# The output projection of a two-part trunk taken tile by tile, with norm, router and ranks behind each tile

## The chip, the cores and the metric

The kernel runs on one core of a Trainium2 chip. The metric is the device time of one execution in microseconds (us). The core has five engines that run their own instruction lists in order and wait for each other by semaphores: TensorE (PE, matmuls), VectorE (DVE), ScalarE (ACT), GpSimd (POOL) and SyncE (SP, which here issues most DMAs).

## The reference

One layer of a decoder trunk over 512 tokens of width 1024. A mixer `m` of three branches ends in a merged `y`, which goes through one output projection; then follow a LayerNorm, a router and a mixture of 16 experts, and a second LayerNorm:

```python
m = einsum('bse,ed->bsd', y, w_o) + b_o
x = layer_norm(ALPHA * x + m, ln1_g, ln1_b)
# hierarchical_moe
group_p = softmax(xf @ w_rg + b_rg)             # 4 groups, the best one
exp_logits = (xf @ w_re + b_re)                 # 4 experts in a group, the best two
gate = sum(one_hot(expert_id) * weights)        # (tokens, 16)
h = einsum('nd,edf->nef', xf, w_up); h_g, h_u = split(h, 2)
h = silu(h_g) * h_u * gate[:, :, None]
f = einsum('nef,efd->nd', h, w_down)
x = layer_norm(ALPHA * x + f, ln2_g, ln2_b)
```

## The kernel before

The 512 tokens are four tiles `t` of 128 rows (`NT` = 4). All large matmuls are done in three passes on operands that are split into a rounded part and a rest: ACT copies the rounded half (`hi`), DVE subtracts it from the source (`lo`).

The output projection has eight pieces `i`, a piece being one tile and one half of the columns, of 24 matmuls each: `wo_mm` (L787). `wo_add` (L794) adds the residual from PSUM on DVE, `wo_stats` takes the statistics of these 512 columns, `r_tr` (L804) transposes the piece on PE, `router` multiplies it with the router's weights. LN1 of a tile (`ln1_stats`, `center_ops`, `scale_ops`), its logits (`logits_a`, `logits_b`), the choice of group and experts (`route_ops`, which ends in the write of `cnt`), the ranks of the tokens within their experts (`rank_mm` on PE, `pos_ops` on DVE) and the selection of the first expert's tokens (`pick`, PE) need both halves of the tile. `put_x1` stores a finished tile to DRAM by two DMAs on SP, where the gathers (`gather`, L1082) of later experts fetch rows by index through POOL. `weave` alternates two lists of operations on an engine. The loop stands at L910; piece `i` is tile `i % 4`, column half `i // 4`.

Expert weights come as three units of 1 MB: 0 and 1 are the up weights, 2 the down weights. `load_unit` (L729) issues a unit on SP and picks its buffer by counting: up units go to the pool `rawx` (two buffers) or `o`, down units to `raw3` (one buffer) or `raw`. `prep_hi` and `prep_lo` (L756, L765) split the up weights into tiles of the pools `xp` and `hlp`, alternating by expert; `dn_hi` and `dn_lo` (L1198, L1203) split the down weights. Expert 0 here is the first in the order of work.

The experts are worked in 18 blocks (`for b in range(nb)`): up matmuls (`up_mm`, L1167), gate, transposes, down matmuls. The result of a block is scattered into one of two accumulators in DRAM, `acc_d[0]` and `acc_d[1]`, by POOL. The last blocks' results stay on the chip (`down_split`, into a tile of `xp`), and are added at the end.

At the end SP loads the rows of LN2's scale and shift into a `raw3` tile (L1388, issued in the last block but one), then three tiles of one accumulator (`acc_load`, L1241); POOL adds the other accumulator to them with DMAs (L1243); `combine` (L1440) adds the last blocks on PE and DVE (L1449), and LN2 follows. All engines run their lists in the order of the code; nothing is reordered at run time.

Of the kernel before, what the change touches and what calls it, by code (L numbers as in the profile page):

```python
# [9 lines left out]
F32 = mybir.dt.float32  # L10
# [43 lines left out]
def trunk(ctx, tc, x, mem, rows, cols, wz, wkv, pac, pb8, pb2, wax, ws, wo, wr, br, we, out):  # L54
# [650 lines left out]
    def load_xr(i):  # L705
        n, t = divmod(i, NT)
        xrs[i] = so2.tile([P, 512], F32, name="xr2") if i % 3 == 2 else so.tile([P, 512], F32, name="xr", bufs=2)
        act.dma_start(xrs[i], xr_d[t * P:(t + 1) * P, n * 512:(n + 1) * 512])
# [20 lines left out]
    def load_unit(key, u):  # L729
        if u < 2:  # L730
            c = counts["up"]
            counts["up"] += 1
            if c % 7 > 4 and key < E:
                t = mox.tile([P, 2048], F32, name="rawx", bufs=2)
            else:
                t = op_.tile([P, 2048], F32, name="o")
        else:
            c = counts["dn"]
            counts["dn"] += 1
            if c % 3 == 1 and key < E:  # L740
# [15 lines left out]
    def prep_hi(key, i):  # L756
        if i == 0:
            counts["prep"] += 1
            wus[key] = []
            pools[key] = xp if counts["prep"] % 2 and key < E else hlp  # L760
        t = pools[key].tile([P, 2, 1024], F32R, name="hl")
        act.copy(t[:, 0], raws[key, i // 2][:, (i % 2) * 1024:(i % 2 + 1) * 1024])  # L762
        wus[key].append(t)
# [18 lines left out]
    for e, u in ((1, 0), (1, 1), (1, 2), (2, 0), (2, 2)):  # L782
        load_unit(e, u)
# [3 lines left out]
    def wo_mm(i, ps, k0, k1):  # L787
        n, t = divmod(i, NT)
        for k in range(k0, k1):
            w = wos[2 * n + k // 4]  # L790
            c = max(t - 2, 0) * P
            mm3(ps, lambda s: yh[min(t, 2)][:, s, k, c:c + P], lambda s: w(s, k % 4), k == 0, k == KD - 1)

    def wo_add(i, ps):  # L794
        n, t = divmod(i, NT)
        dve.tensor_tensor(x1[:, t, n * 512:(n + 1) * 512], ps, xrs[i], op=ALU.add)

    def wo_stats(i):
        n, t = divmod(i, NT)
# [4 lines left out]
    def r_tr(i):  # L804
        n, t = divmod(i, NT)
# [7 lines left out]
    def router(i):  # L813
        n, t = divmod(i, NT)
# [95 lines left out]
    rest = []  # L910
    pending = {NT: [(2, 1)], NT + 1: [(3, 0), (3, 1)], NT + 2: [(4, 0)]}
    for i in range(2 * NT):
        j = i - 1
        t = j - NT
        ps = mmps()
        if i == 6:
            ohe = so2.tile([P, NT, P], F32, name="xr2")
        wo_mm(i, ps, 0, 2)
        if i:
            r_tr(j)  # L920
        if i in (NT + 1, NT + 2):
            for h in range(2):
                prep_hi(0, 2 * (i - NT - 1) + h)
        wo_mm(i, ps, 2, 4)
        if i:
            router(j)
        if t == 0:
            weave(ln1_stats(0))
        elif t == 1:
            weave(ln1_stats(1), scale_ops(0, 256, range(0, D, 256)))  # L930
            put_x1(sp, 0)
        elif t == 2:
            ops, r_ = route_ops(0, 2)
            rest += r_
            weave(ops, ln1_stats(2))
        if t >= 0:
            logits_a(t)
            weave(center_ops(t, D, (0,)))
            logits_b(t)
            if t:  # L940
                weave(scale_ops(t, 512, (0, 512)))
                put_x1(sp, t)
        wo_mm(i, ps, 4, 6)
        if t == 2:
            rank_mm(0)
            rank_mm(1)
            ops, r_ = route_ops(2, 3)
            rest += r_
            weave(ops, pos_ops(0, 2)[:2])
        wo_mm(i, ps, 6, 8)  # L950
# [54 lines left out]
    prep_hi(1, 0)  # L1005
    prep_hi(1, 1)
# [147 lines left out]
    load_unit(4, 1)  # L1154

# [154 lines left out]
    for b in range(nb):  # L1310
# [3 lines left out]
        if b == 0:  # L1314
            dn_hi(0, 0)
# [287 lines left out]
```

## Time and profile before

| | |
|---|---|
| median of three runs | 927.21 us (923.76 to 929.75) |
| profiled execution | 924.31 us, span 922.6 us |
| PE, DVE, ACT, POOL busy | 878.1, 586.4, 462.5, 91.2 us |
| mean DMA rate | 160 GB/s |
| output projection to expert 0 | 641 to 708.5 us |
| experts' blocks | to about 883 us |

A profile shows one execution; times in it are microseconds from the span's start. A row of a timeline gives start and length of an instruction (or of a run of alike ones, with their count), its engine, its line in the code and out<-in by the names of tiles, and in brackets the idle time of the engine before it with what ended it.

### The profile page before, as it was taken

To read this page: it belongs to the slowest core of one execution; us is meant where nothing else is said; L and a number is where in the kernel's file an instruction comes from. 1 tells how busy PE (TensorE), PEld (TensorE's weight loads), DVE (VectorE), ACT (ScalarE), POOL (GpSimd) and SP (SyncE) were. 2 spreads that over 40 slices of the span, in tenths; PEclk is the share of its full clock that TensorE was granted. 3 is DMA by queue.
4 is the path that set the end of the run, shared out by engine and by line. 5 is a ranking of instruction groups with operands and counts; after the bars stand their busy time and mean duration, and the time that the engine had idled before them with its cause. 6 is when DMAs were issued, how large, how long until landed. Compare 5 with 4: busy or idle time off the path is not lost.

```text
span 922.6 us, 11201 instructions
## 1 busy us (share of the span) xinstructions
PE 878.1 (95%) x4272; PEld 729.4 (79%) x4272; DVE 586.4 (64%) x995; ACT 462.5 (50%) x658; POOL 91.2 (10%) x86
## 2 busy tenths in 40 slices
PE   8999999999999999999999999999987889999990
PEld 5778888889998888888788888788866778888870
DVE  6755773344555543345866775765288987689966
ACT  5545432223454442215678687433124667679852
POOL 0000100000000100000000000000001123233943
PEclk9999999999999999999999999999999999999995
DMA  8313633323222612321313331338573888899582
GB/s 336 124 46 114 223 120 109 115 96 128 102 92 98 226 49 103 117 80 64 114 58 103 137 103 58 115 124 339 228 277 118 282 309 288 249 314 394 170 184 104
DMA packets 29871, 147.85 MB, mean 160 GB/s; under 512 B 5539, under 2 KB 5795, under 8 KB 16756
## 3 DMA queue, kind: packets, MB, share of 16 engines
q1 hardware_dynamic: 21316, 127.77, 37.8%
q0 software_dynamic: 7056, 17.12, 7.2%
q10 hardware_dynamic: 1440, 2.19, 0.7%
q8 instruction: 35, 0.57, 0.3%
q14 instruction: 24, 0.20, 0.1%
HBM read 137.29 MB, written 18.35 MB: 169 GB/s over the span
## 4 chain that ended last, share of the span: by engine, by line
PE 74%; DVE 11%; DMA 5%; ACT 4%; POOL 3%; issue 2%; SPq 0%; POOLq 0%; ACTq 0%; DVEq 0%
PE mm L109 60%; PE aux L109 4%; PE mm L307 3%; PE mm L1221 3%; DVE hl L768 2%; POOL rawx L1255 2%; DMA y<-acc_d 1%; DMA o<-in_we_dram 1%; DMA x<-in_x_dram 1%; DMA col<-in_cols_dram 1%; PE aux L1163 1%; DVE hl L83 1%; PE aux L463 1%; DMA acc_d<-yb,ix_x 1%; ACT hl L82 1%
## 5 line engine op out<-in xcount | busy, mean ns | idle before, releaser
L109 PE MATMUL mm<-hl 128*128 128x512 f32 x1416 | 327.7, 390 | 0.2 <-DVE hl L83 0.2
L109 PEld LDWEIGHTS mm<-hl 128*128 128x128 f32 x1416 | 264.6, 188 | 54.7 <-DVE hl L83 0.6
L83 DVE TENSOR_TENSOR hl<-raw,hl 128x1024 fp32r<-128x1024 f32 (+1 forms) x116 | 136.2, 1181 | 136.4 <-ACT hl L82 135.8
L82 ACT CAST hl<-raw 128x1024 fp32r<-128x1024 f32 (+1 forms) x116 | 116.3, 1014 | 126.1 <-PE mm L109 113.7
L109 PE MATMUL mm<-o,hl 128*128 128x512 f32 x624 | 142.9, 389 | 1.2 <-ACT o L82 1.2
L109 PEld LDWEIGHTS mm<-o,hl 128*128 128x128 f32 x624 | 117.1, 188 | 25.9 <-ACT o L82 1.6
L109 PE MATMUL mm<-hl,xs 128*128 128x512 f32 x432 | 105.1, 399 | 1.1 <-DVE xs L83 1.1
L109 PEld LDWEIGHTS mm<-hl,xs 128*128 128x128 f32 x432 | 80.7, 191 | 18.1 <-DVE xs L83 1.9
L768 DVE TENSOR_TENSOR hl<-o,hl 128x1024 fp32r<-128x1024 f32 (+1 forms) x52 | 57.8, 1143 | 2.0 <-ACT hl L762 1.9
L1221 PE MATMUL mm<-hl,hT 128*128 128x512 f32 x196 | 49.8, 400 | 0.8 <-DVE hT L83 0.8
L762 ACT CAST hl<-o 128x1024 fp32r<-128x1024 f32 x48 | 48.1, 1054 | 1.7 <-PE mm L1221 1.7
L1085 POOL DMA_INDIRECT y<-x_d,ixg x3 | 3.2, 1058 | 402.7 <-DVE rtl L1144 402.1
L1221 PEld LDWEIGHTS mm<-hl,hT 128*128 128x128 f32 x196 | 35.5, 188 | 7.9 <-DVE hT L83 1.2
L223 ACT ACTIVATE gate<-mm,col 128x512 f32<-128x512 f32 x24 | 16.5, 688 | 39.6 <-PE mm L109 39.5
L1210 DVE TENSOR_TENSOR hl<-raw,hl 128x1024 fp32r<-128x1024 f32 x26 | 30.8, 1225 | 3.5 <-PE mm L109 1.9
L1201 ACT CAST hl<-raw 128x1024 fp32r<-128x1024 f32 x32 | 31.9, 1053 | 0.0
L109 PE MATMUL mm<-memT,hl 128*128 128x256 f32 x192 | 27.3, 286 | 0.2 <-ACT memT L82 0.2
L810 ACT COPY x1T<-aux 128x512 f32<-128x512 f32 x8 | 4.7, 588 | 43.6 <-PE aux L809 23.6
L307 PE MATMUL mm<-o,hl 128*128 128x512 f32 x96 | 25.2, 409 | 1.1 <-ACT hl L82 0.4
L109 PEld LDWEIGHTS mm<-memT,hl 128*128 128x128 f32 x192 | 24.9, 191 | 0.9 <-ACT memT L82 0.4
L1085 POOL DMA_INDIRECT y<-x_d,ix_x x13 | 17.8, 1370 | 70.7 <-PE aux L1163 67.4
L109 PE MATMUL mm<-hl,yh 128*128 128x512 f32 x96 | 24.6, 400 | 0.0
(342 smaller groups left out, 1170.6 us busy)
## 6 DMA issues: line engine op xcount, KB each, us to landing
raw<-in_wz_dram SPq DMA_DIRECT2D x30, 1024.0 KB, 4.7
o<-in_we_dram SPq DMA_DIRECT2D x24, 1024.0 KB, 7.9
raw<-in_we_dram SPq DMA_DIRECT2D x16, 1024.0 KB, 6.6
raw<-in_pac_dram SPq DMA_DIRECT2D x8, 1024.0 KB, 4.6
raw<-in_wkv_dram SPq DMA_DIRECT2D x8, 1024.0 KB, 4.7
rawx<-in_we_dram SPq DMA_DIRECT2D x8, 1024.0 KB, 6.8
raw<-in_pb_dram SPq DMA_DIRECT2D x4, 1024.0 KB
raw<-in_wo_dram SPq DMA_DIRECT2D x4, 1024.0 KB, 4.8
```

Of the source, the lines that this page charges most:

```text
L82: act.copy(hi, src)
L83: dve.tensor_tensor(lo, src, hi.bitcast(F32), op=ALU.subtract)
L109: pe.matmul(ps, lhsT=a(sa_), rhs=b(sb_), start=first and i == 0, stop=last and i == 2)
L223: act.activation(store[j], ps, AF.Sigmoid, bias=cc(C_M + br_i * 8 + j))
L307: pe.matmul(ps, lhsT=xT(k, slice(t * P, (t + 1) * P))(sx), rhs=wv[2 * n + k // 4, k // 2 % 2][:, sw, k % 2, :], start=i == 0, stop=i == 23)
L762: act.copy(t[:, 0], raws[key, i // 2][:, (i % 2) * 1024:(i % 2 + 1) * 1024])
L768: (eng or dve).tensor_tensor(t[:, 1, c0:c1], src[:, c0:c1], t[:, 0, c0:c1].bitcast(F32), op=ALU.subtract)
L1085: pool.indirect_dma_start(out=xg, out_offset=None, in_=x1_d[:, :], in_offset=bass.IndirectOffsetOnAxis(ap=ix[:, b:b + 1], axis=0), bounds_ ...
L1201: act.copy(dnh[key][:, :, n * 512:(n + 1) * 512], dn_half(key, n))
L1210: eng.tensor_tensor(dnl[key][n], dn_half(key, n), dnh[key][:, :, ns].bitcast(F32), op=ALU.subtract)
L1221: pe.matmul(ps, lhsT=hT[:, sa_, f, :], rhs=dn[sb_][:, f, :], start=i + f == 0, stop=i + f == 3)
L1255: pool.tensor_scalar(t_[:, t * P:(t + 1) * P], iof, float(t * P), ixf, op0=ALU.add, op1=ALU.is_equal)
```

## The change

The pieces of the output projection are taken tile by tile: piece `i` is now tile `i // 2`, column half `i % 2`. The norm, the router's choice and the ranks of a tile follow the tile's second half, in the loop. Expert 0's raw up weights are loaded into the pool `raw`, and their rounded parts go to `o` tiles, one quarter in each of the iterations 1 to 4 (before: two quarters each in the iterations 5 and 6, `o` to `xp`). Before the loop SP loads only expert 0's units, the rows of LN1 and one unit of expert 1; four more units are issued in the iterations 4 and 5, and five behind the first expert's up matmuls. The rules by which `load_unit` and `prep_hi` choose a pool change their phase.

```diff
     def load_xr(i):
-        n, t = divmod(i, NT)
+        t, n = divmod(i, 2)
...
-            if c % 7 > 4 and key < E:
+            if key == 0:
+                t = rawp.tile([P, 2048], F32, name="raw")
+            elif c % 7 in (3, 4) and key < E:
                 t = mox.tile([P, 2048], F32, name="rawx", bufs=2)
...
-            if c % 3 == 1 and key < E:
+            if c % 3 == 0 and key < E:
                 t = mlate.tile([P, 2048], F32, name="raw3")
...
-            pools[key] = xp if counts["prep"] % 2 and key < E else hlp
-        t = pools[key].tile([P, 2, 1024], F32R, name="hl")
+            pools[key] = op_ if key == 0 else hlp if counts["prep"] % 2 or key >= E else xp
+        t = pools[key].tile([P, 2, 1024], F32R, name="hl" if key else "o")
...
-    for e, u in ((1, 0), (1, 1), (1, 2), (2, 0), (2, 2)):
-        load_unit(e, u)
+    load_unit(1, 0)
...
-    pending = {NT: [(2, 1)], NT + 1: [(3, 0), (3, 1)], NT + 2: [(4, 0)]}
+    pending = {4: [(1, 1), (2, 0)], 5: [(1, 2), (2, 2)]}
+
+    def ln1_tile(t, fill=()):
+        weave(ln1_stats(t), fill)
+        logits_a(t)
+        weave(center_ops(t, 512, (0, 512)))
+        logits_b(t)
+
+    def mm_pair(i, ps, q):
+        wo_mm(i, ps, 2 * q, 2 * q + 2)
+
     for i in range(2 * NT):
         j = i - 1
-        t = j - NT
         ps = mmps()
+        mm_pair(i, ps, 0)
...
         if i:
             r_tr(j)
-        if i in (NT + 1, NT + 2):
-            for h in range(2):
-                prep_hi(0, 2 * (i - NT - 1) + h)
-        wo_mm(i, ps, 2, 4)
+        if 0 < i < 5:
+            prep_hi(0, i - 1)
+        mm_pair(i, ps, 1)
         if i:
             router(j)
-        if t == 0:
-            weave(ln1_stats(0))
...
+        if i and i % 2 == 0:
+            t = i // 2 - 1
+            ln1_tile(t)
+            weave(scale_ops(t, 512, (0, 512)))
+            put_x1(sp, t)
+        if 0 < i < 5:
+            prep_lo(0, i - 1)
+        if i == 5:
+            ops, rest = route_ops(0, 2)
+            weave(ops)
+        mm_pair(i, ps, 2)
+        if i == 5:
             rank_mm(0)
             rank_mm(1)
...
+        if i == 6:
+            weave(pos_ops(0, 2) + rest)
+        if i == 7:
+            ops, rest = route_ops(2, 3)
+            weave(ops)
+        mm_pair(i, ps, 3)
         for e, u in pending.get(i, ()):
             load_unit(e, u)
+        if i == 7:
+            rank_mm(2)
         wo_add(i, ps)
         wo_stats(i)
-        if i in (NT + 1, NT + 2):
-            for h in range(2):
-                prep_lo(0, 2 * (i - NT - 1) + h)
...
     r_tr(2 * NT - 1)
-    rank_mm(2)
-    weave(ln1_stats(t), pos_ops(0, 2)[2:] + pos_ops(2, 3) + rest)
     pick(1, 0, 4)
+    prep_hi(1, 0)
+    prep_hi(1, 1)
     router(2 * NT - 1)
+    ln1_tile(t, pos_ops(2, 3))
     pick(1, 4, 8)
-    logits_a(t)
-    logits_b(t)
-    ops, rest = route_ops(t, NT)
-    weave(ops, center_ops(t, 512, (0, 512)) + scale_ops(t, 512, (0, 512)))
+    pick(2, 0, 8)
+    ops, rest3 = route_ops(t, NT)
+    weave(ops, scale_ops(t, 256, range(0, D, 256)))
     put_x1(sp, t)
-    pick(2, 0, 4)
     rank_mm(t)
-    pick(2, 4, 8)
     weave(pos_ops(t, NT))
     pick(t, 0, 8)
+    weave(rest)
+    rest = rest3
...
-    load_unit(4, 1)
...
         if b == 0:
+            for e, u in ((2, 1), (3, 0), (3, 1), (4, 0), (4, 1)):
+                load_unit(e, u)
             dn_hi(0, 0)
```

SP's list in the output projection, from the last load ahead of the loop. `in_we_dram` holds the expert weights, `x_d` the normed tiles, `acc_d` the first accumulator. Before:

```order
L751 DMA rawx<-in_we_dram 128x2048 x2
L751 DMA o<-in_we_dram 128x2048
L908 DMA x_d<-y 128x1024
L908 DMA acc_d<-y 128x1024
L908 DMA x_d<-y 128x1024
L908 DMA acc_d<-y 128x1024
L751 DMA o<-in_we_dram 128x2048
L908 DMA x_d<-y 128x1024
L908 DMA acc_d<-y 128x1024
L908 DMA x_d<-y 128x1024
L908 DMA acc_d<-y 128x1024
L751 DMA o<-in_we_dram 128x2048
```

Now:

```order
L753 DMA o<-in_we_dram 128x2048
L909 DMA x_d<-y 128x1024
L909 DMA acc_d<-y 128x1024
...
L753 DMA rawx<-in_we_dram 128x2048 x2
L753 DMA raw<-in_we_dram 128x2048 x2
L909 DMA x_d<-y 128x1024
L909 DMA acc_d<-y 128x1024
...
L753 DMA o<-in_we_dram 128x2048 x5
```

The stores of the first two tiles now stand ahead of the loads of the loop, and five loads follow the last store in a row.

DVE's list in the loop, from the addition of the seventh piece. Before (`hl<-o,hl` is expert 0's rounding, the L894 to L133 rows the variance of LN1, the rows from L851 the choice of experts):

```order
L796 TENSOR_TENSOR y<-mm,xr 128x512
L802 BN_STATS bnst_4874<-y 128x6
L768 TENSOR_TENSOR hl<-o,hl 128x1024 x2
L894 BN_AGGR bnmv<-bnst_4874 128x2
L851 TENSOR_TENSOR scr_4754<-ge 128x32
L124 TENSOR_SCALAR lnv_5133<-bnmv 128x1
L853 TENSOR_TENSOR scr_4754<-scr_4754,thr 128x32
L126 TENSOR_SCALAR lnr_5134<-lnv_5133 128x1
```

Now, from its addition of the seventh piece:

```order
L797 TENSOR_TENSOR y<-mm,xr 128x512
L803 BN_STATS bnst_5139<-y 128x6
L852 TENSOR_TENSOR scr_4746<-ge 128x16
L854 TENSOR_TENSOR scr_4746<-scr_4746,thr 128x16
L856 TENSOR_REDUCE rk<-scr_4746 128x4
...
L866 TENSOR_TENSOR cnt<-r_4750,goh 128x16
L797 TENSOR_TENSOR y<-mm,xr 128x512
L803 BN_STATS bnst_5139<-y 128x6
L895 BN_AGGR bnmv<-bnst_5139 128x2
```

Between the last two additions now stands only the choice of experts of one tile; the rounding and the norm that stood there have gone ahead.

SP's and DVE's lists at the end, with the numbers of the tiles. `raw3_6779` is the fourteenth expert's down weights, `raw_6969` and, in the change, `raw3_6972` the last one's; `in_rows_dram` holds the rows of LN2. SP before:

```order
L751 DMA raw3_6779<-in_we_dram 128x2048
...
L751 DMA raw_6873<-in_we_dram 128x2048
...
L751 DMA raw_6969<-in_we_dram 128x2048
L1388 DMA raw3_7103<-in_rows_dram 128x1024 x2
L1241 DMA y_7159<-acc1_d_96 128x1024 x3
```

DVE before:

```order
L1210 TENSOR_TENSOR hl_7066<-raw3_6779,hl_7064 128x2x512 x2
...
L1210 TENSOR_TENSOR o_7177<-raw_6969,hl_7174 128x2x512
L1178 SCALAR_TENSOR_TENSOR h_7179<-h_7179,gw_x_5891,mm_7131 128x256
L83 TENSOR_TENSOR rawx_6911<-aux_7189,rawx_6911 128x256
L1210 TENSOR_TENSOR o_7177<-raw_6969,hl_7174 128x2x512
```

SP now:

```order
L753 DMA raw3_6677<-in_we_dram 128x2048
...
L753 DMA raw_6876<-in_we_dram 128x2048
...
L753 DMA raw3_6972<-in_we_dram 128x2048
L1389 DMA raw3_7106<-in_rows_dram 128x1024 x2
L1240 DMA y_7162<-acc1_d_96 128x1024 x3
```

DVE now:

```order
L1209 TENSOR_TENSOR o_7173<-raw_6876,hl_7171 128x2x512 x2
L1209 TENSOR_TENSOR o_7180<-raw3_6972,hl_7177 128x2x512
L1177 SCALAR_TENSOR_TENSOR h_7182<-h_7182,gw_x_5894,mm_7134 128x256
L83 TENSOR_TENSOR rawx_6914<-aux_7192,rawx_6914 128x256
L1209 TENSOR_TENSOR o_7180<-raw3_6972,hl_7177 128x2x512
```

The single `raw3` buffer into which the rows of LN2 go was last read by DVE's rounding of the fourteenth expert, and is now last read by that of the last expert, at the end of DVE's rows above.

## Rows read from the trace of the kernel before

**Rows 1.** Windows: length, busy of PE, PEld, DVE, ACT, POOL (count), PEclk, DMA share, GB/s.
```profile
641.00:670.00 29.00, 29.00 (x156) 24.60 (x154) 7.10 (x18) 4.49 (x11) 0.00 (x0) 1.00 0.67 268
670.00:695.00 25.00, 19.25 (x106) 15.66 (x107) 22.52 (x73) 4.11 (x6) 0.00 (x0) 1.00 0.72 270
720.00:743.00 23.00, 18.73 (x94) 14.88 (x92) 22.62 (x61) 13.48 (x22) 3.60 (x2) 1.00 0.85 309
743.00:842.00 99.00, 99.00 (x484) 82.39 (x485) 79.89 (x98) 72.75 (x109) 30.52 (x21) 0.98 0.87 299
```

**Rows 2.** Timeline of PE, output projection and routing: start, length, what, [idle before].
```profile
640.58 0.60 PE L809 MATMUL aux<-ident,y 128*128 128x128 f32 x4
647.39 0.60 PE L809 MATMUL aux<-ident,y 128*128 128x128 f32 x4
683.76 0.66 PE L809 MATMUL aux<-ident,y 128*128 128x128 f32 x4 [2.06 <-DVE y L796]
689.25 1.63 PE L109 MATMUL mm<-hl,yh 128*128 128x512 f32 x6
703.32 4.39 PE L889 MATMUL mm<-xr,y 128*128 128x128 f32 x24
708.54 5.90 PE L109 MATMUL mm<-hl,xs 128*128 128x512 f32 x24
```

**Rows 3.** Timeline of DVE over the same stretch.
```profile
646.23 0.69 DVE L796 TENSOR_TENSOR y<-mm,xr 128x512 f32<-128x512 f32 x1 [5.39 <-PE mm L109]
668.16 0.21 DVE L894 BATCH_NORM_AGGREGATE bnmv<-bnst 128x2 f32<-128x12 f32 x1
670.10 1.28 DVE L899 SCALAR_TENSOR_TENSOR y<-y,bnmv,g 128x1024 f32<-128x1024 f32 x1
674.86 2.34 DVE L768 TENSOR_TENSOR hl<-o,hl 128x1024 fp32r<-128x1024 f32 x2
681.69 1.41 DVE L903 SCALAR_TENSOR_TENSOR y<-y,lnr,b 128x512 f32<-128x512 f32 x2
694.27 0.68 DVE L796 TENSOR_TENSOR y<-mm,xr 128x512 f32<-128x512 f32 x1
703.06 0.18 DVE L865 TENSOR_TENSOR cnt<-r,goh 128x16 bf16<-128x16 f32 x1
717.92 1.28 DVE L83 TENSOR_TENSOR xs<-aux,xs 128x512 fp32r<-128x512 f32 x2
```

**Rows 4.** Line L1085, the gathers: issue on POOL and time to landing, whole run.
```profile
L1085 POOL DMA_INDIRECT y<-x_d,ixg x3: 1001/1073/1099, 710.9 to 713.7; - x3
DMA to landing us min/median/max: 5.9/6.4/8.9
```

**Rows 5.** Timeline of PE: the second expert's transposes.
```profile
715.12 1.06 PE L1163 MATMUL aux<-ident,y 128*128 128x128 f32 x8 [0.69 <-DMA y<-x_d,ixg]
```

**Rows 6.** Timeline of SP, PE, ACT, DVE and POOL at the end of the kernel.
```profile
871.22 1.10 SPq L1388 DMA_DIRECT2D raw<-in_rows_dram  x2
873.74 1.28 SPq L1241 DMA_DIRECT2D y<-acc_d  x3
876.44 5.71 PE L109 MATMUL mm<-hl,xs 128*128 128x512 f32 x24
875.52 0.64 ACT L82 CAST hl<-mm 128x512 fp32r<-128x512 f32 x1
884.51 1.22 DVE L1210 TENSOR_TENSOR o<-raw,hl 128x1024 fp32r<-128x1024 f32 x1
885.78 1.88 POOL L1243 DMA_DIRECT2D y<-acc_d  x2 [4.97 <-DMA acc_d<-yb,ix_x]
891.65 0.69 DVE L1449 SCALAR_TENSOR_TENSOR y<-aux,y 128x512 f32<-128x512 f32 x1 [2.44 <-DMA y<-acc_d]
898.26 0.69 DVE L1449 SCALAR_TENSOR_TENSOR y<-aux,y 128x512 f32<-128x512 f32 x1 [2.67 <-DMA y<-acc_d]
```

**Rows 7.** Line L1241, the accumulator loads: time to landing.
```profile
DMA to landing us min/median/max: 6.5/6.5/6.5
```

More of the change, by code (lines that the diff above doesn't have):

```diff
@@ L787, in wo_mm @@
     def wo_mm(i, ps, k0, k1):
-        n, t = divmod(i, NT)
+        t, n = divmod(i, 2)
         for k in range(k0, k1):
@@ L794, in wo_add @@
     def wo_add(i, ps):
-        n, t = divmod(i, NT)
+        t, n = divmod(i, 2)
         dve.tensor_tensor(x1[:, t, n * 512:(n + 1) * 512], ps, xrs[i], op=ALU.add)
     def wo_stats(i):
-        n, t = divmod(i, NT)
+        t, n = divmod(i, 2)
         if n == 0:
@@ L804, in r_tr @@
     def r_tr(i):
-        n, t = divmod(i, NT)
+        t, n = divmod(i, 2)
         x1T = so.tile([P, 4, P], F32, name="x1T", bufs=1)
@@ L813, in router @@
     def router(i):
-        n, t = divmod(i, NT)
+        t, n = divmod(i, 2)
         ps = auxps()
@@ L825, in logits_b @@
     def logits_b(t):
-        dve.tensor_tensor(ge[:, t, :], ge[:, t, :], routed[NT + t][:, :20], op=ALU.add)
+        dve.tensor_tensor(ge[:, t, :], ge[:, t, :], routed[2 * t + 1][:, :20], op=ALU.add)
         dve.scalar_tensor_tensor(ge[:, t, :], ge[:, t, :], rstds[t], cv, op0=ALU.mult, op1=ALU.add)
@@ L908, in put_x1 @@
             eng.dma_start(d_[t * P:(t + 1) * P, :], x1[:, t, :])
-    rest = []
-    pending = {NT: [(2, 1)], NT + 1: [(3, 0), (3, 1)], NT + 2: [(4, 0)]}
+    pending = {4: [(1, 1), (2, 0)], 5: [(1, 2), (2, 2)]}
[6 more added lines that the diff above has]
+        wo_mm(i, ps, 2 * q, 2 * q + 2)
     for i in range(2 * NT):
         j = i - 1
-        t = j - NT
@@ L915, in trunk @@
         ps = mmps()
+        mm_pair(i, ps, 0)
         if i == 6:
             ohe = so2.tile([P, NT, P], F32, name="xr2")
-        wo_mm(i, ps, 0, 2)
         if i:
             r_tr(j)
-        if i in (NT + 1, NT + 2):
-            for h in range(2):
-                prep_hi(0, 2 * (i - NT - 1) + h)
-        wo_mm(i, ps, 2, 4)
+        if 0 < i < 5:
+            prep_hi(0, i - 1)
+        mm_pair(i, ps, 1)
         if i:
             router(j)
-        if t == 0:
-            weave(ln1_stats(0))
[L929 to L935, printed above, removed]
@@ L936, in trunk @@
-        if t >= 0:
-            logits_a(t)
-            weave(center_ops(t, D, (0,)))
-            logits_b(t)
[L940 to L944, printed above, removed]
+        if i and i % 2 == 0:
[8 more added lines that the diff above has]
+            weave(ops)
@@ L945, in trunk @@
+        mm_pair(i, ps, 2)
+        if i == 5:
             rank_mm(0)
             rank_mm(1)
[L947 to L950, printed above, removed]
+        if i == 6:
[4 more added lines that the diff above has]
+        mm_pair(i, ps, 3)
         for e, u in pending.get(i, ()):
             load_unit(e, u)
+        if i == 7:
+            rank_mm(2)
@@ L963, in trunk @@
     r_tr(2 * NT - 1)
-    rank_mm(2)
-    weave(ln1_stats(t), pos_ops(0, 2)[2:] + pos_ops(2, 3) + rest)
     pick(1, 0, 4)
+    prep_hi(1, 0)
+    prep_hi(1, 1)
     router(2 * NT - 1)
+    ln1_tile(t, pos_ops(2, 3))
     pick(1, 4, 8)
-    logits_a(t)
-    logits_b(t)
-    ops, rest = route_ops(t, NT)
-    weave(ops, center_ops(t, 512, (0, 512)) + scale_ops(t, 512, (0, 512)))
+    pick(2, 0, 8)
+    ops, rest3 = route_ops(t, NT)
+    weave(ops, scale_ops(t, 256, range(0, D, 256)))
     put_x1(sp, t)
-    pick(2, 0, 4)
     rank_mm(t)
-    pick(2, 4, 8)
     weave(pos_ops(t, NT))
     pick(t, 0, 8)
+    weave(rest)
+    rest = rest3
     rtl = rt0.tile([P, 7, NT], F32, name="rtl")
@@ L1004, in trunk @@
     ]
-    prep_hi(1, 0)
-    prep_hi(1, 1)
     weave(first)
```

## The prediction

> **What bounds the kernel now.** I read the stages first, by the windows of busy time [rows 1]. From 743 to 842, which is typical of the experts' blocks up to 883, TensorE (PE) is busy 99.00 of 99 us: whatever makes the first of these matmuls earlier makes the end earlier by as much, as long as nothing behind them is late. From 641 to 670, the first half of the output projection, PE is busy 29.00 of 29. Then from 670 to 695 only 19.25 of 25: here PE waits, and VectorE (DVE) is busy 22.52 of 25. From 720 to 743, expert maps and first experts, DVE has 22.62 of 23. So the program is bound by PE, with two stretches that belong to DVE, and its end, after 883, is a chain of waits over DMAs.
>
> The timeline of PE gives the loop's clock: the four transposes of one piece start at 640.58, those of the next at 647.39, a period of 6.81 us for the 24 matmuls of a piece with its small work [rows 2]. Where column half 1 brings norm and router, PE idles 2.06 before the transposes at 683.76, for DVE's addition (L796). The last six matmuls end at 689.25 + 1.63 = 690.88, but DVE adds the last piece only at 694.27 [rows 2, 3]: expert 0's rounding (2.34 for two), the norm and the ranks stand in its queue. The count of tile 3 ends at 703.06 + 0.18 = 703.24, and expert 0's first up matmul runs at 708.54 [rows 2, 3].
>
> At the end SyncE (SP) issues the rows of LN2 at 871.22 and three accumulator loads at 873.74, and GpSimd (POOL) adds the second accumulator with DMAs from 885.78; DVE waits for these before the first, 2.44 us at 891.65, and the third tile, 2.67 us at 898.26 [rows 6]. The loads of SP take 6.5 us to land [rows 7], so they lie at 873.74 + 6.5 = 880.2, 5.5 us before POOL wants them. That cover is the second thing that the change touches.
>
> **The output projection, tile by tile.** The 192 matmuls are the same; with the period 6.81 from 640.58, the transposes of the eighth piece stand at 640.58 + 7 x 6.81 = 688.25 if DVE keeps up. The addition starts 1.16 before the transposes (646.23 against 647.39 [rows 2, 3]), 0.69 of it its own, so DVE has a slack of 0.47 in each piece. DVE's work in an even iteration is now: addition 0.69 and the statistics of the same 512 columns, which I take alike; the variance chain 668.16 to 670.10, 1.94; the centring 1.28; three small operations on the logits at 0.18 (the row of the count is the nearest); the scaling 1.41; and one of expert 0's subtractions, half of 2.34 [rows 3]. That is 0.69 + 0.69 + 1.94 + 1.28 + 0.54 + 1.41 + 1.17 = 7.72, against 6.81: 0.91 too much, less the slack 0.47 is 0.44. It comes three times (iterations 2, 4, 6; the last has positions for the subtraction, which I count alike), 1.3 us. The odd iterations hold only the addition and a subtraction, or the ranks, and give DVE time to catch up. The eighth addition then starts at 688.25 - 1.16 + 1.3 = 688.4, not 694.27: **5.9 us earlier**. Bounds: 7.2 with no stall, and 1.0 if each of the three costs the 2.06 of idle time that the old order shows once [rows 2] (6.2 in all). I take 5.9, since DVE's own durations make it up.
>
> **From the eighth addition to expert 0.** The way over norm, router, logits and ranks of the last tile to its count took 694.27 to 703.24, 9.0 us. Its parts remain, with fewer filler operations between them; I take 9.0 again. From the count to expert 0's first matmul were 703.24 to 708.54, 5.3 us, held by the 24 selection matmuls of 4.39 [rows 2]. Now the eight of tile 2 go ahead of tile 3's count, so I take 4.4, with 3.8 and 5.3 as ends. Expert 0 starts at 688.4 + 9.0 + 4.4 = 701.8, **6.7 earlier**. The rounding of expert 1's first halves on ScalarE goes ahead too and costs nothing, since ScalarE is busy 13.48 of 23 even in the stretch behind [rows 1].
>
> **The loads.** Five units of 1 MB, 5.2 MB in all, now leave SP behind expert 0's matmuls instead of inside the loop; expert 0's units go to the raw pool and its rounded ones into "o" tiles, so these loads wait for PE's use of those tiles, up to 708. They meet the gather of expert 1's rows: issued at 710.9 before, with its transposes at 715.12, 4.2 later [rows 4, 5], hence issued at 704.2 now. DVE's subtraction of these rows came at 717.92 [rows 3], now due at 711.2. Gathers took 5.9, 6.4 and 8.9 us by the view of their line [rows 4]. With 6.4 and 1.2 for transposes (1.06) and cast, 704.2 + 6.4 + 1.2 = 711.8, **0.6 late**; the ends are 0 and 3.1 (at 8.9). Behind that, the stretch to 743 keeps its DVE work and PE its matmuls, so 6.7 - 0.6 = **6.1** arrives at the blocks. The unit (2,1), wanted by ScalarE at about 712, is issued near 703.5 and lands just in time; the other moved ones are wanted from 725 on.
> [...] The row with 8.9 shows that a gather may take 3 us longer than its neighbour, so I keep the range.
>
> **The end.** Now the parity: the units of the down weights that go to the single raw3 buffer are now the first, fourth, ... sixteenth instead of the second, ... fourteenth. So the last expert's down weights lie in the buffer into which LN2's rows are loaded next. Before, that buffer came free with the fourteenth's rounding, and SP issued at 871.22; now SP must wait for the second half of the last expert's rounding on DVE, 884.51 + 1.22 = 885.73 [rows 6]. I take 886.5: ScalarE's cast at 875.52 now writes into a tile that the last expert's up weights hold, and waits for six of the 24 matmuls from 876.44, up to 876.44 + 5.71 / 4 = 877.9 [rows 6]; of these 2.4 us the rounding, which has slack, gets a third. What is queued behind SP's wait: the three accumulator loads, since SP goes in order; and behind those POOL's adding loads; and behind those DVE. The sum, on the old time axis: rows issued from 886.5, 1.10 for two; first accumulator load at 887.6, landed 6.5 later [rows 7] at 894.1; POOL starts at 894.1 instead of 885.78, **8.3 later**. Everything from there to the end hangs on these DMAs (DVE waited for them with nothing else to do, at 891.65 and 898.26 [rows 6]), so all of it arrives. The lower end is 7.0: rows issued at 885.73 and a load that lands in 5.9, like the fastest gather [rows 4]. The upper is 9.7: the loads had a lead of 2.5 us over the rows ahead of them (871.22 to 873.74), now 1.1, and the other 1.4 is waited for.
> [...] The row has 6.5, and it is for this very load.
>
> **The sum.** The profiled execution took 924.31, with a span of 922.6 and 1.7 around it: 924.3 - 6.1 + 8.3 = 926.5. It lies 2.9 below the median of 927.21, so the forecast is 927.2 + 2.2 = **929** (rounded down from 929.4), with a range of its own from 926.5 to 935: front gain 2 to 7.5 (the ends of its terms don't all come together), loss 7.0 to 9.7. About 1%, 9.3 us, is what a measurement of this kernel can tell from no change, so this is "the same".
>
> **The rivals.**
> 1. The end costs nothing: the rows' load finds its buffer free, or the accumulators land while POOL still waits for the last scatter. For it: POOL did wait, 4.97 us, for a scatter [rows 6]. Against: that wait ended at 885.78, and SP can't issue before the rounding that ends there. Time 924.3 - 6.1 = 918.2, on the median 921. Chance 0.13.
> 2. Slower, by the burst of loads: the gather and the weights stand behind 5.2 MB, which at 299 GB/s [rows 1] take 17.5 us, up to 721. Expert 1's rows would come some 10 us after their due time 711.2, PE and DVE idle, and the gain of 6.7 becomes a loss of 3.3: 924.3 + 3.3 + 8.3 = 935.9, 939 on the median. It decides against the kernel when the gather lands over 6 us late. For it: the 8.9 us. Against: the gathers landed within 9 us though SP's loads ran beside them (309 GB/s from 720 to 743). Chance 0.12. [...]
> 3. The gain at the front doesn't come: DVE's queue holds the loop at every tile, and the old 694.27 is met again. Time 924.3 + 8.3 = 932.6, 935.5 on the median. Against: DVE's work in the loop isn't more than before, and PE ran 19.25 of 25. Chance 0.10.
>
> My forecast has the remaining 0.65.
>
> **How the numbers follow.** The range 920.5 to 937.5 takes in most of rival 1, rival 3 and the lower part of rival 2; about 0.17 is left out. Faster by over 1% (under 918) needs rival 1 with the front gain at its upper end or a term that I don't see: 0.08. Slower by over 1% (over 936.5): most of rival 2, and the upper part of rival 3: 0.15. Within 1%: 0.77.
>
> **What would show it.** The eighth addition at about 688.4 and expert 0's first matmul at 701.8; no idle time of PE over 1 us in the loop; the first gather landing by 711; steady blocks 6 us earlier. At the end, SP's rows issued only after the last rounding, near 880, the accumulator loads right behind, POOL's first adding load at about 894.1 - 6.1 = 888, and DVE waiting some 8 us more than before at the first combine. I am wrong if SP issues the rows early, if POOL's start doesn't move with the accumulators' landing, or if the front gain is outside 2 to 7.5.

## The result and the profile after

The changed kernel takes 932.95 us in the median of 20 runs (925.17 to 934.36), the kernel before 925.8 (20 runs, 923.39 to 929.75). The ratio is 1.0057, with a 95% interval from 1.0041 to 1.0072: slower by about half a per cent. The times of the changed kernel lie in two groups, fifteen between 931.9 and 934.4 and five between 925.2 and 929.1; that is why the ratio is smaller than that of the medians. In the longer group the mean granted clock of TensorE in each run is 0.975 to 0.977, in the shorter 0.978 to 0.980. The profiled execution took 932.28, with a span of 930.6, and belongs to the longer group.

The timeline of PE in the changed kernel, around the first experts (start, length, instruction, idle time before it):

```profile
640.49 0.60 PE L810 MATMUL aux<-ident,y 128*128 128x128 f32 x4
...
682.50 0.66 PE L810 MATMUL aux<-ident,y 128*128 128x128 f32 x4
...
701.17 5.75 PE L109 MATMUL mm<-o,xs 128*128 128x512 f32 x24
712.34 1.94 PE L1162 MATMUL aux<-ident,y 128*128 128x128 f32 x8 [5.42 <-DMA y<-x_d,ixg]
...
715.64 7.65 PE L109 MATMUL mm<-hl,xs 128*128 128x512 f32 x24
...
727.98 5.73 PE L109 MATMUL mm<-hl,xs 128*128 128x512 f32 x24
...
741.66 8.24 PE L109 MATMUL mm<-hl,xs 128*128 128x512 f32 x24
...
754.40 5.72 PE L109 MATMUL mm<-hl,xs 128*128 128x512 f32 x24
```

The same places in the kernel before that [rows 2, 5] don't have:

```profile
723.79 0.38 PE L1184 MATMUL aux<-ident,h 128*128 128x128 f32 x2
...
729.84 5.71 PE L109 MATMUL mm<-hl,xs 128*128 128x512 f32 x24
...
743.36 7.33 PE L109 MATMUL mm<-hl,xs 128*128 128x512 f32 x24
...
755.19 5.72 PE L109 MATMUL mm<-hl,xs 128*128 128x512 f32 x24
```

And on DVE, SP and POOL in the changed kernel: the eighth addition, tile 3's count, the burst of five loads, the gather of expert 1's rows, and DVE's subtraction of these rows:

```profile
688.25 0.69 DVE L797 TENSOR_TENSOR y<-mm,xr 128x512 f32<-128x512 f32 x1 [2.94 <-PE aux L878]
...
696.68 0.18 DVE L866 TENSOR_TENSOR cnt<-r,goh 128x16 bf16<-128x16 f32 x1
...
714.09 0.69 DVE L83 TENSOR_TENSOR xs<-aux,xs 128x512 fp32r<-128x512 f32 x1 [3.58 <-ACT xs L82]
```

```profile
702.86 5.28 SPq L753 DMA_DIRECT2D o<-in_we_dram  x5
703.39 1.10 POOL L1086 DMA_INDIRECT y<-x_d,ixg  x1 [394.74 <-ACT hl L764]
```

The loop did what was forecast. The transposes wait for DVE nowhere by much: the six periods from 640.49 to 682.50 take 42.0 us, 1.15 more than six times the 6.81 of [rows 2] (1.3 forecast), and the idle time of 2.06 at 683.76 in [rows 2] has gone. The eighth addition starts at 688.25 (688.4 forecast), the count ends at 696.86 (697.4) and expert 0's matmuls start at 701.17 (701.8; 708.54 in [rows 2]). So expert 0 is 7.37 us earlier. Then PE waits 5.42 us for the gather. DVE has expert 1's rows at 714.09, against 717.92 in [rows 3]: of the 7.37 there are 3.83 left. The reader should follow the same instruction in both kernels: the transposes after expert 1's matmuls stand at 723.13 now (0.16 before 715.64 + 7.65 = 723.29, since the two rows overlap) and at 723.79 before, 0.66 left; block 2 at 727.98 and 729.84, 1.86 (before, DVE held PE in between); block 3 at 741.66 and 743.36, 1.70; block 4 at 754.40 and 755.19, **0.79**. The matmuls of expert 1 took 7.65, where those of block 2 take 5.73, and those of block 3 8.24 instead of 7.33.

The windows tell why matmuls got longer (length, busy time of PE, PEld, DVE, ACT, POOL with counts, granted clock, DMA share, GB/s). Before:

```profile
712.00:728.00 16.00, 13.42 (x70) 10.61 (x69) 15.49 (x46) 9.40 (x15) 3.35 (x3) 1.00 0.81 267
743.00:752.00 9.00, 9.00 (x41) 7.54 (x42) 8.32 (x12) 5.15 (x7) 2.70 (x2) 0.81 0.81 274
```

After:

```profile
712.00:728.00 16.00, 14.98 (x65) 12.65 (x65) 11.94 (x34) 8.03 (x13) 1.00 (x1) 0.76 1.01 420
743.00:752.00 9.00, 9.00 (x41) 7.45 (x40) 6.66 (x9) 4.06 (x7) 2.26 (x3) 0.78 0.86 287
```

The granted clock behind PE's wait is 0.76 of full speed over 712 to 728, where it was 1.00. In steps of 2 us it is 1.00 up to 708, 0.87 from 708 to 710 and 0.50 from 710 to 718: here it falls while PE waits. From the transposes of expert 1 (712.34, before 715.12) to those behind its matmuls (723.13, before 723.79) the stretch takes 10.79 us at the lower clock, against 8.67: 2.1 of the 2.8 us that had been left, although PE waited 1.11 for DVE in that stretch before and doesn't now.

The end of the changed kernel, on SP, POOL and DVE, answers to [rows 6]:

```profile
886.09 0.81 SPq L1389 DMA_DIRECT2D raw<-in_rows_dram  x2
887.14 1.55 SPq L1240 DMA_DIRECT2D y<-acc_d  x3
```

```profile
893.38 1.92 POOL L1242 DMA_DIRECT2D y<-acc_d  x2 [13.37 <-DMA y<-acc_d]
```

```profile
884.81 1.22 DVE L1209 TENSOR_TENSOR o<-raw,hl 128x1024 fp32r<-128x1024 f32 x1
...
899.43 0.69 DVE L1450 SCALAR_TENSOR_TENSOR y<-aux,y 128x512 f32<-128x512 f32 x1 [9.91 <-DMA y<-acc_d]
```

In the chain that ended last, the first of the accumulator loads takes:

```profile
887.14 5.68 DMA y<-acc_d
```

SP issues the rows of LN2 at 886.09, where it was 871.22, right behind the rounding of the last expert on DVE (884.81 + 1.22 = 886.03); the accumulator loads follow at 887.14 instead of 873.74, and the first lands 5.68 later; POOL's first adding load moves from 885.78 to 893.38, 7.6 later, and DVE waits 9.91 at its first combine, where it waited 2.44. The span is 8.0 longer.

### The profile page after: what moved, and what is told of

It reads as the page before. It is cut to its first block, busy times and chain, and to the rows that moved or that the text cites. A ratio compares the mean times of both kernels' runs of the same rounds, so it can differ in the third digit from the quotient of the medians.

```text
span 930.6 us, 11201 instructions
## 1 busy us (share of the span) xinstructions
PE 883.3 (95%) x4272; PEld 733.2 (79%) x4272; DVE 588.8 (63%) x998; ACT 462.5 (50%) x658; POOL 89.8 (10%) x86
## 4 chain that ended last, share of the span: by engine, by line
PE 79%; DVE 11%; ACT 4%; DMA 3%; issue 2%; POOL 0%; SPq 0%; POOLq 0%; ACTq 0%; DVEq 0%
PE mm L109 62%; PE mm L1220 4%; PE aux L109 4%; PE mm L307 3%; DMA y<-acc_d 2%; PE aux L1162 2%; DMA y<-x_d,ixg 1%; ACT hl L82 1%; DVE hl L83 1%; PE mm L352 1%; PE aux L463 1%; DVE hl L770 1%; DVE lnr L126 1%; DVE th L687 0%; DVE o L1209 0%
## 5 line engine op out<-in xcount | busy, mean ns | idle before, releaser
L109 PE MATMUL mm<-hl 128*128 128x512 f32 x1416 | 327.6, 390 | 0.2 <-DVE hl L83 0.2
L109 PEld LDWEIGHTS mm<-hl 128*128 128x128 f32 x1416 | 264.6, 188 | 54.7 <-DVE hl L83 0.6
L109 PE MATMUL mm<-o,hl 128*128 128x512 f32 x624 | 142.9, 389 | 1.2 <-ACT o L82 1.2
L109 PEld LDWEIGHTS mm<-o,hl 128*128 128x128 f32 x624 | 117.1, 188 | 25.9 <-ACT o L82 1.6
L109 PE MATMUL mm<-hl,xs 128*128 128x512 f32 x408 | 101.7, 407 | 0.0
L109 PEld LDWEIGHTS mm<-hl,xs 128*128 128x128 f32 x408 | 78.6, 196 | 16.3
L770 DVE TENSOR_TENSOR hl<-o,hl 128x1024 fp32r<-128x1024 f32 (+1 forms) x45 | 50.5, 1151 | 4.8 <-ACT hl L764 4.7
L764 ACT CAST hl<-o 128x1024 fp32r<-128x1024 f32 x42 | 42.0, 1052 | 4.2 <-PE mm L1220 4.2
L109 PE MATMUL mm<-memT,hl 128*128 128x256 f32 x192 | 27.3, 286 | 0.2 <-ACT memT L82 0.2
L109 PEld LDWEIGHTS mm<-memT,hl 128*128 128x128 f32 x192 | 24.9, 191 | 0.9 <-ACT memT L82 0.4
L83 DVE TENSOR_TENSOR xs<-aux,xs 128x512 fp32r<-128x512 f32 x34 | 22.0, 686 | 5.4 <-ACT xs L82 5.4
L109 PE MATMUL mm<-hl,memT 128*128 128x256 f32 x192 | 24.3, 283 | 0.0
```

The lines of the kernel that those rows point to most:

```text
L83: dve.tensor_tensor(lo, src, hi.bitcast(F32), op=ALU.subtract)
L109: pe.matmul(ps, lhsT=a(sa_), rhs=b(sb_), start=first and i == 0, stop=last and i == 2)
L770: (eng or dve).tensor_tensor(t[:, 1, c0:c1], src[:, c0:c1], t[:, 0, c0:c1].bitcast(F32), op=ALU.subtract)
```

## The experiments

The theory after the result has two parts. **The end**: the rows of LN2 wait for the last expert's rounding, and the accumulator loads stand behind them on SP; price about 8. **The front**: the gain of 7.4 is real, but the gather of expert 1's rows meets the burst of five loads, and the clock is lower behind PE's wait for it; by block 4 they have eaten 6.6. That the wait is what brings the clock down is part of the theory, and the experiments don't show it. Rivals stand in the expectations. Ratios are to the kernel before, in the same runs.

**1. The last unit back in the raw pool**, in the changed kernel:

```diff
-            if c % 3 == 0 and key < E:
+            if c % 3 == 0 and c < 15 and key < E:
```

> The changed kernel, but the last expert's down weights go to the raw pool as they did before, so the single raw3 buffer comes free for the rows of LN2 after the thirteenth expert. Theory of the end (the rows' load waits for the last rounding, and the accumulator loads behind it): SP issues the rows near 862 to 871 instead of 886.1, POOL's first adding load goes back from 893.4 to about 885.2, and the time falls by 8.0, from 933.0 to 925. Rival (that wait is not what holds POOL, the last scatter is): POOL stays near 893 and the time within 1 us of 933.

Measured: 925.19 (10 runs, 923.7 to 926.7), ratio 0.9997 (0.9981 to 1.0013). SP and POOL at the end:

```profile
870.81 0.84 SPq L1389 DMA_DIRECT2D raw<-in_rows_dram  x2
872.88 1.34 SPq L1240 DMA_DIRECT2D y<-acc_d  x3
```

```profile
885.29 1.88 POOL L1242 DMA_DIRECT2D y<-acc_d  x2 [5.34 <-DMA acc_d<-yb,ix_x]
```

The 8 us come back, by an edit of one buffer's choice: the span is 922.7, 7.9 less than in the changed kernel's profile, and POOL's first adding load is 8.1 earlier. (By the ratios it is 0.6%, 5.6 us, since those of the changed kernel take in its shorter group.) The front is as in the changed kernel (expert 1's transposes at 712.18), so what is left of the change brings nothing that can be measured; the span before is 922.6.

**2. The other way round**: the kernel before with that rule alone.

```diff
-            if c % 3 == 1 and key < E:
+            if c % 3 == 0 and key < E:
```

> The kernel before with one rule of the change alone: raw3 takes the first, fourth, ... sixteenth down unit. Theory of the end: SP's rows of LN2 at about 885.7 instead of 871.2, POOL's first adding load at about 893.3 instead of 885.8, the time 925.8 + 7.6 = 933.4. Rival (the loss comes from the front or needs the moved parity of the up weights as well): 925.8, within 1 us.

Measured: 933.22 (4 runs, 931.2 to 935.1), ratio 1.0085 (1.0054 to 1.0116). With the old front:

```profile
885.26 0.81 SPq L1388 DMA_DIRECT2D raw<-in_rows_dram  x2
886.31 1.47 SPq L1241 DMA_DIRECT2D y<-acc_d  x3
```

```profile
892.71 1.88 POOL L1243 DMA_DIRECT2D y<-acc_d  x2 [12.44 <-DMA y<-acc_d]
```

The rule alone makes the loss, 6.9 us here by the medians and the profiles, 7.9 by the ratio; neither the front nor the parity of the up weights is needed.

**3. What is it that waits?** In the changed kernel the accumulator loads go to SP ahead of the rows, which still wait.

```diff
-            load_gb(sp, 0)
-            load_gb(sp, 1)
...
     acc_load((nb + 1) % 2, 2, sp)
+    load_gb(sp, 0)
+    load_gb(sp, 1)
```

> The changed kernel with the three accumulator loads issued on SP ahead of the two loads of LN2's rows; the rows still wait for the last rounding in the same buffer. Theory of the end (it is the loads queued behind the wait that cost, not the late rows): accumulator loads near 873, POOL's first adding load near 885.3 instead of 893.4, the rows at 886 land by 893, before POOL's first use of them near 898; the time 925, like the kernel with the last unit in the raw pool. Rival (the late rows themselves delay LN2): 928 to 933.

Measured: 927.41 (10 runs, six at 927.3 to 928.6 and four at 920.8 to 923.4), ratio 0.9996 (0.9968 to 1.0023).

```profile
873.06 2.26 SPq L1240 DMA_DIRECT2D y<-acc_d  x3
886.20 0.82 SPq L1389 DMA_DIRECT2D raw<-in_rows_dram  x2
```

```profile
885.28 1.88 POOL L1242 DMA_DIRECT2D y<-acc_d  x2 [5.16 <-issue]
...
898.63 0.86 POOL L1242 DMA_DIRECT2D y<-acc_d  x1 [10.02 <-DMA y<-acc_d]
```

POOL's first adding load is back at 885.28. So most of the loss is the queue behind the wait. But the rows, two loads of 512 KB, now leave at 886.20, in the stretch of POOL's own loads (from 885.28 on): the last adding load starts at 898.63 after a wait of 10.02, where the first experiment has 895.88 and 7.25. With the same front (expert 1's transposes at 712.32 and 712.18) the span is 925.8, 3.1 more than there, and the median is 2.2 more. The expectation was right about POOL's start; the rival, that the late rows cost something themselves, holds for the smaller part.

**4. The burst later**, in the changed kernel: SP reads the table of experts' numbers first, which DVE has ready at 708.2.

```diff
         if b == 0:
+            regs[NSTAT] = sp.value_load(blk["eid"][0:1, 0:1], min_val=0, max_val=E - 1)
             for e, u in ((2, 1), (3, 0), (3, 1), (4, 0), (4, 1)):
                 load_unit(e, u)
```

> The changed kernel, but SP reads the table of experts' numbers (ready at 708.2) before the five loads of 1 MB behind expert 0's matmuls, so they leave at about 708.5 instead of 702.9. Theory of the gather (the burst holds expert 1's rows back): the gather's transposes stand some 4.2 after its issue, at about 707.6 instead of 712.3, PE's idle time of 5.4 falls under 1.5, expert 1's matmuls start at 710 to 711 instead of 715.6, and nearly the whole 7.4 of the front arrives at the blocks: the time falls by 6 to 7, to 926 to 927. Rival one (DVE's maps and rounding up to 743 decide, the gather hides there): PE's idle time goes but the time falls by at most 2, to 931. Rival two (the gather is slow by itself, here because its rows were just stored): transposes stay near 712, time 933.

Measured: 927.77 (10 runs, 926.7 to 929.1), ratio 1.0017 (1.0002 to 1.0033), 5.2 less than the changed kernel's median. The gather of expert 1's rows on POOL, PE, and the window of the clock:

```profile
704.19 1.10 POOL L1086 DMA_INDIRECT y<-x_d,ixg  x1 [395.70 <-DVE rtl L1145]
```

```profile
701.84 5.89 PE L109 MATMUL mm<-o,xs 128*128 128x512 f32 x24
708.84 1.06 PE L1162 MATMUL aux<-ident,y 128*128 128x128 f32 x8 [1.11 <-DMA y<-x_d,ixg]
...
711.96 8.03 PE L109 MATMUL mm<-hl,xs 128*128 128x512 f32 x22 [0.57 <-DVE xs L83]
...
724.67 5.74 PE L109 MATMUL mm<-hl,xs 128*128 128x512 f32 x24
```

```profile
712.00:728.00 16.00, 15.32 (x61) 12.22 (x62) 14.03 (x46) 8.60 (x13) 1.80 (x2) 0.82 0.98 398
```

The wait is down to 1.11. From the gather's issue to the transposes of its rows it is 4.65 us (704.19 to 708.84), against 8.95 in the changed kernel (703.39 to 712.34) and 4.2 before [rows 4, 5]. Block 2 starts 5.2 earlier than before (729.84). Rivals one and two fall. The times lie in one group. In this execution the clock is low again in expert 1's matmuls, 8.03 for 22 of them, and less arrives than the 6 to 7 expected. It is 0.87 over 695 to 712 and 0.82 over 712 to 728, and PE's waits before these matmuls are 1.11 and 0.57: here the clock fell without a wait of 5.4.

**5. Both edits** (1 and 4).

> Both edits together. If the two losses stand apart, their sum: 933.0 - 8.0 - 6.5 = 918.5, a ratio of 0.992 to the kernel before. If the loads that leave later are missed by the rounding behind, or the front's gain is lost again in the blocks: 922 to 925.

Measured: **919.26** (6 runs, 917.2 to 920.2), ratio 0.9925 (0.9902 to 0.9948), faster than both kernels. PE, and the window of the clock:

```profile
700.99 5.73 PE L109 MATMUL mm<-o,xs 128*128 128x512 f32 x24
708.03 1.06 PE L1162 MATMUL aux<-ident,y 128*128 128x128 f32 x8 [1.31 <-DMA y<-x_d,ixg]
...
711.04 5.29 PE L109 MATMUL mm<-hl,xs 128*128 128x512 f32 x22 [0.59 <-DVE xs L83]
...
722.63 5.73 PE L109 MATMUL mm<-hl,xs 128*128 128x512 f32 x24
```

```profile
712.00:728.00 16.00, 14.00 (x67) 11.10 (x67) 15.29 (x46) 9.77 (x15) 1.62 (x1) 1.00 1.01 418
```

7.2 us of the front arrive at block 2, and the median is 7.0 below that of the kernel before. The gather is as in experiment 4; here the 22 matmuls take 5.29 at a clock of 1.00. That is the price of the clock by two rows with nearly the same waits (why it fell in one of the two is not shown): 8.03 - 5.29 = 2.7 on PE, of which some 1.2 reach block 2 (2.04 less the 0.85 that expert 0 was later), since PE at full clock waits 1.21 for ScalarE instead. The two losses add, by the medians: 932.95 - 7.8 - 5.2 = 920, measured 919.3.

**6. How the gather is slowed.** Two of the five loads at once, three after the table:

```diff
         if b == 0:
-            for e, u in ((2, 1), (3, 0), (3, 1), (4, 0), (4, 1)):
+            load_unit(2, 1)
+            load_unit(3, 0)
+            regs[NSTAT] = sp.value_load(blk["eid"][0:1, 0:1], min_val=0, max_val=E - 1)
+            for e, u in ((3, 1), (4, 0), (4, 1)):
                 load_unit(e, u)
```

> The changed kernel with two of the five loads behind expert 0's matmuls at once and three after the table of experts' numbers (708.2). Theory of the gather: its wait grows with the bytes that are queued when it starts, so 2 MB (5 us at the 400 GB/s of that stretch) from 702.9 let the rows land at about 709 to 710, between the 708.8 without and the 712.3 with all five loads; PE idles 2 to 3, and the time is 927.5 to 930. Rival (any load of SP ahead of the gather holds it as long as five do): transposes at 712, 933.

Measured: 932.25 (10 runs, three at 925.4 to 926.5 and seven at 931.2 to 935.5), ratio 1.0048 (1.0019 to 1.0078): the expectation by bytes was wrong. The gather, issued at 705.24, keeps PE waiting as long as with all five:

```profile
714.31 1.94 PE L1162 MATMUL aux<-ident,y 128*128 128x128 f32 x8 [5.53 <-DMA y<-x_d,ixg]
```

The DMA queues show what moved. In the changed kernel, from 708 to 710, SP's queue (q1) and POOL's (q0) have these packets, MB and shares of the DMA engines' time:

```profile
q1 hardware_dynamic: 59, 0.48, 60.2%
q0 software_dynamic: 67, 0.27, 32.9%
```

In this step and the next two, both queues moved about as many packets (78 and 80 from 710 to 712, 75 and 74 from 712 to 714). By these figures a packet of the gather carries 0.27 MB / 67 = 4 KB and one of the weights 0.48 MB / 59 = 8 KB, and POOL's queue moved 0.27, 0.27 and 0.30 of 0.75, 0.82 and 0.87 MB, about a third; in experiment 4, with nothing of SP's beside it, it moved 0.54 MB from 706 to 708. In experiment 6 itself the numbers are 63 and 69 from 710 to 712, but 81 and 41 in the step before and 56 and 122 in the step after, and in the changed kernel they are 78 and 27 from 706 to 708, so equal numbers are not shown as a rule. Here SP's queue moved 0.11, 0.58, 0.53, 0.52 and 0.35 MB in steps of 2 us from 704 to 714, so its first two loads, 2.1 MB, took until about 714 (the other three left from 711.0 on, behind them), and the gather landed 8.9 after its issue, at 714.1. That two loads hold the gather as long as five because they last as long as it does is the author's reading of these steps.

**7. One load at once, four later**, the same edit with (2, 1) alone ahead of the table.

> The changed kernel with one of the five loads (2,1) at once and four after the table of experts' numbers. In the half burst the gather was as late as with all five, so the bytes queued are not what counts. Theory of the share (while SP's queue has packets, POOL's queue moves about a third of the bytes, and all of them once SP's is empty): 1 MB is through near 707.5, the gather shares for some 2 us only and its transposes stand at 709 to 710, PE idles 1.5 to 2.5, the time is 927.5 to 929.5. Rival (any load of SP in front makes the gather late by 4): transposes at 712, 932 to 933.

Measured: 926.83 (10 runs, six at 925.5 to 927.1 and four at 929.8 to 930.7), ratio 1.0032 (1.0013 to 1.0051). None of the ten times lies in the 927.5 to 929.5 that the share gave; the rival's 932 to 933 falls. The profile, of the shorter group, doesn't test the share, but shows another thing, on PE, SP and POOL:

```profile
701.89 7.40 PE L109 MATMUL mm<-o,xs 128*128 128x512 f32 x24
709.13 1.03 PE L1162 MATMUL aux<-ident,y 128*128 128x128 f32 x8
```

```profile
704.83 6.30 SPq L753 DMA_DIRECT2D o<-in_we_dram  x5
```

```profile
703.42 1.10 POOL L1086 DMA_INDIRECT y<-x_d,ixg  x1 [394.87 <-DVE rtl L1145]
```

Here expert 0's matmuls ran at a lower clock (0.80 over 695 to 712), 7.40 us instead of 5.75. The first load waits for PE to finish with a tile (in the changed kernel's trace SP waits 5.4 us for L109 before it), and so left at 704.83 instead of 702.86, behind the gather at 703.42; and the gather's rows were there without a wait. So here the slow PE let the gather go first. What that is worth in time is not shown, since no execution of the longer group was profiled.

**8. PE kept busy in the wait**, in the changed kernel: 22 more matmuls of expert 0's rows with themselves, into a tile that nobody reads.

```diff
+            wps = auxps()
+            for k in range(22):
+                pe.matmul(wps, lhsT=xsm[0][:, 0, k % 8, :], rhs=xsm[0][:, 0, 0:4, :].rearrange("p k n -> p (k n)"), start=k == 0, stop=k == 21)
             transp(1)
```

> The changed kernel with 22 extra matmuls of 128x512 (on expert 0's rows, into a tile that nobody reads) between expert 0's matmuls and expert 1's transposes, some 5.2 us in which PE waits for the gather anyway. Theory of the clock (the wait brings the granted clock down, and expert 1's work then runs at the lower one: transposes 1.94 instead of 1.06, matmuls 7.65 instead of 5.72): the granted clock from 712 to 728 is 1.00 instead of 0.76, the matmuls of expert 1 take about 5.7, and the time falls by 2 to 4, from 933 to 929 to 931. Rival (the clock falls for another reason, or DVE's work hides it): the clock or the time stays, 932 to 934.

Measured: 930.95 (8 runs, 929.6 to 933.5), ratio 1.0059 (1.0037 to 1.0081).

```profile
702.42 7.63 PE L109 MATMUL mm<-o,xs 128*128 128x512 f32 x24
709.89 5.15 PE L1320 MATMUL aux<-xs 128*128 128x512 f32 x22
714.88 1.03 PE L1162 MATMUL aux<-ident,y 128*128 128x128 f32 x8
...
716.56 5.75 PE L109 MATMUL mm<-hl,xs 128*128 128x512 f32 x24
```

The median is in the expected range, though the ratio is that of the changed kernel (1.0057), and expert 1's matmuls take 5.75. But this execution had the low clock already in expert 0 (7.63; 0.80 over 695 to 712), with SP's loads at 705.36, and the gather, issued at 704.00, landed after 4.9; PE then did the extra matmuls for nothing. So it doesn't test whether the wait brings the clock down, nor its price; that stays open.

**9. The two groups of times.** The changed kernel once more, and the kernel of experiment 3 twice more.

> The changed kernel as it is, for a second profile, since five of its 20 times were 925 to 929 and the rest 931.9 to 934.4. Theory: where the gather meets less of the burst, or the clock stays up, the time is 925 to 929, and the wait before the transposes of expert 1 or the matmuls behind it are shorter; else a profile like the first with 932 to 934.

> The kernel with the accumulator loads first, once more, for a profile of its shorter executions (4 of its 10 times were 920.8 to 923.4, the others 927.3 to 928.6). If the gather decides between the two: in a time near 921 the transposes of expert 1 come 708 to 710 and the first long matmuls behind them take about 5.7. If it is the clock alone: transposes at 712, with the granted clock at 1.00 from 712 to 752. If it is the end: the same front as in the first profile and an earlier last accumulator load.

> The same kernel a third time, for the same purpose: near 921 the profile shows which of the gather, the clock and the end is different from the first one; near 928 it repeats it.

Measured: 933.42 in the median of three (926.13, 933.42, 933.61), the profiled one 933.61; 928.29; 928.72. All three profiles are of the longer group, with PE's wait of 5.62, 5.56 and 5.45 before expert 1's transposes. What the shorter group does is therefore **not shown** in these kernels. Experiments 7 and 8 show a way that might give it: a gather that is issued ahead of the first load. It fits that both kernels whose burst waits for the table (4 and 5) have one group; against it, the ten times of experiment 1 have one group too, with the burst in place, and the profile of experiment 8 has the gather ahead in an execution of 932.23, one of the longer of its eight. Which matmuls meet the low clock also changes from execution to execution: up to expert 0's matmuls these kernels are alike, and over 695 to 712 the clock is 0.87, 0.90, 0.80 and 0.80 in the profiles of experiments 4, 6, 7 and 8, 1.00 in that of experiment 5, and 0.93 in those of the changed kernel and of experiments 1 and 3 (the first). In the changed kernel it is 1.00 up to 708; in experiment 6 it is 0.91 already from 688 to 701, in experiment 3 (the first) 1.00 there. Expert 0's matmuls take 7.40 and 7.63 in 7 and 8, and 5.73 to 5.89 in the others named here.

## Why the prediction was right in the time and wrong in a term

- **The loop and the way to expert 0: right.** 688.25 against 688.4, 696.86 against 697.4, 701.17 against 701.8: 7.4 us earlier where 6.7 were forecast. DVE's overhang cost 1.15 in the loop by 682.50, of the 1.3 forecast.
- **The loads: the term that failed.** The prediction put the gather "0.6 late" and let 6.1 "arrive" at the blocks. Its 6.4 was not the first gather's: [rows 4] has the least, middle and greatest landing time of that line in the whole run, not one for each of the three gathers. The first took 4.2 from its issue to the transposes of its rows, by the prediction's own 710.9 and 715.12, so with that price it would have been in time. Beside the burst it took 8.95, 4.7 more. Expert 1's rows reached DVE 3.5 behind the time that the front gave them (717.92 - 7.37 = 710.55, and 714.09); 3.1 had been named as the end. And the sum had no term for the clock behind that, 0.76, which took most of what remained. So 0.8 us arrived at block 4, and at the end nothing (spans of 922.7 in experiment 1 and 922.6 before). Experiments 4 and 5 show the burst's part: without it at the gather's start, 5.2 and 7.2 arrive at block 2. What brings the clock down is not shown.
- **Rival 2: half right.** Rival 2 was right that the burst delays the gather, and wrong in its form: when the rows landed, at 712.2, SP's queue had moved 2.2 of the 5.2 MB.
- **The end: right.** SP issues at 886.09, where 886.5 less the front's remainder of 0.8 is 885.7. The first load landed in 5.68 for 6.5. POOL starts 7.6 later on the trace's own axis; against experiment 1, which has the same front, it starts 8.1 later and the span is 7.9 longer, where 8.3 was forecast. Experiments 1 and 2 give 7.8 and 6.9 for this one rule by the medians.
- **The sum, and luck.** -6.1 + 8.3 = 2.2 was forecast. In the profiles the front gave nothing and the end cost 8, and the span is 8.0 longer; the change costs 7.2 by the medians and 5.3 by the ratio, since a quarter of the runs are in the shorter group. The prediction had named a front gain outside 2 to 7.5 as a sign of being wrong, and that sign was met. The time fell into the range because it was wide enough for a front without a gain: that is rival 3's sum, 932.6 against the 932.28 of the profile. But rival 3 loses the gain in the loop, where it came in full. That the time is right is luck as far as the front goes.

## What to carry to other kernels

A rule that deals buffers out by counting touches every later user of these buffers: look at what is loaded last into the pool and which instruction now frees it, and what stands behind that load on the same queue. When a phase gets earlier, its consumers' DMAs get earlier too and may meet a burst that is triggered by the same event; a transfer that somebody waits for should be issued before it, or the burst should be made to wait for something a little later (here, in experiment 4, the gather's rows were transposed 4.65 us after its issue instead of 8.95). Matmuls that run at a lower clock have a price of their own beside PE's waits: here 2.7 us for 22 matmuls (8.03 and 5.29, in windows at 0.82 and 1.00), of which 1.2 reached the next block.

## What the runs showed of the hardware that was not expected

In the changed kernel the queues of SP and POOL moved about equal numbers of packets in three steps of 2 us from 708 to 714: 59 and 67, 78 and 80, 75 and 74. In experiment 6 it was 63 and 69 from 710 to 712, but 81 and 41 before that and 56 and 122 after it. From 708 to 710 of the changed kernel the gather of 4 KB rows, beside loads of 8 KB packets, got 0.27 of 0.75 MB. From its issue to the transposes of its rows it took 8.95 with such a neighbour (the changed kernel) and 4.65 without (experiment 4); its landing was 4.9 when it started ahead (experiment 8). And in experiment 7 a lower clock of PE (0.80 over 695 to 712) turned the order of two transfers: with 7.40 instead of 5.75 for expert 0's matmuls, the first of the loads that wait for PE left at 704.83, behind the gather at 703.42, and PE's wait of 5.4 was gone. Whether that makes a kernel faster is not shown.
